# Three edits around the expert part of a decoder layer: stores of h2 and x1 from GpSimd's queue, a bank for each first tile, columns for each index product

## The chip, the cores and the metric

The kernel runs on one core of a Trainium2 chip. The metric is the device time of one execution in microseconds. A core has five engines that run side by side, each through its own list of instructions in order: TensorE (PE, matmul), VectorE (DVE), ScalarE (ACT), GpSimd (POOL) and SyncE (SP). They meet at semaphores. SyncE and GpSimd also issue transfers (DMAs), which 16 DMA engines carry out. Matmul results go to eight banks.

## The reference

The layer takes 512 tokens of 1024 channels. A mixer (a state-space branch and a forgetting-attention branch, merged by gates) is followed by a layer norm; its result is `x1`. A modulated norm of it, `h2`, goes to a mixture of 16 experts: a router picks one of four groups for each token and two experts in it.

```
for e in range(N_EXPERTS):
    hid = jax.nn.silu(t @ w_gate[e]) * (t @ w_up[e])
    out = out + gates[:, e:e + 1] * (hid @ w_down[e])
```

Here `t` holds rows of h2, an expert has 512 hidden channels, and the output is the layer norm of ALPHA times x1 plus the gated sum of the experts.

## The kernel before

Up to about 540 us the kernel computes the modulation and the mixer; the change does not touch that part. What follows is the router and the experts.

**Rows of h2 and x1.** Tokens come in four blocks of 128 rows. For blocks 0 to 2, `norms(i)` computes h2 and stores it to `h2d` in device memory, `keep_x1(i)` scales x1 and stores it to `moed`, both from SyncE's queue. For block 3 this is done by `keep_x1(3)` and `last_h2()`. SyncE's queue also issues the loads of expert weights (`ew.load`, L358): pieces of 1 MB into a ring of 19 pieces, six for an expert (two of gate, two of up, two of down). A piece is loaded again when `drop` frees it.

**Setup.** `setup_experts()` lays out the experts' buffers over memory that earlier parts leave free; GpSimd fills seven of them with zeros (L1130). Some lie where block 3's h2 rows were, and must wait for these rows' store.

**Tokens of a tile.** An expert's tokens are taken in tiles of 64. `tokens()` finds them: small matmuls of one-hot rows (L1149, L1151; "index products") give the row numbers and gates of a tile in columns 128 to 132 of bank 7. VectorE turns them into an index (L1153) and adds up the gate (L1158); GpSimd gathers the rows from `h2d` by an indirect transfer (L1154). `x_columns` transposes them (L1173, L1174).

**An expert's tile.** `body(e, t)` multiplies with gate and up weights (`up`, L1278) into bank 0 for an even t and bank 1 for an odd one, applies the activation (`hidden`), multiplies the tile before it with its down weights (`down`, L1293), scales the result (`add`, L1297) and scatters it onto `moed` by an indirect transfer that adds (L1298), transposes the hidden values (`hidden_columns`, L1287), and at t = 0 makes the index products of the expert after next. Tile 0 is always run; tiles 1 and 2 stand under branches on the expert's count (L1344, L1346). In this run's data ten experts have one tile, four have two and two have three. The work of further tiles (`over`) isn't run.

**Order.** A scheduler orders each engine's list by what it takes to be ready. Inside `in_order(...)` the order of TensorE, VectorE and ScalarE is that of the code. At a branch each engine reads the count and jumps for itself; on the path that skips tiles TensorE first waits for its own matmuls.

The end (L1405 on) loads `moed` again, normalises it and stores the output from GpSimd (L1423).

Of the kernel before, what the change touches and what calls it, by code (L numbers as in the profile page):

```python
# [14 lines left out]
ALU = mybir.AluOpType  # L15
AX = mybir.AxisListType

P = 128
# [89 lines left out]
def hybrid_layer(ctx: ExitStack, tc: tile.TileContext, A, out):  # L108
    nc = tc.nc
# [3 lines left out]
    banks = [psp.tile([P, 512], F32, name=f"bank{i}") for i in range(8)]  # L113
# [9 lines left out]
    h2d = tc.dram_tile([S, D], F32, name="h2d")  # L123
    moed = tc.dram_tile([S + P, D], F32, name="moed")
# [68 lines left out]
    for hh in range(2):  # L193
        half = slice(hh * 64, (hh + 1) * 64)
# [209 lines left out]
    for j in range(4):  # L404
        raws = [mod_pair(j, kh) for kh in range(2)] if j else mod0
        acc = FM.alloc(1)
        for k in range(KT):
            r = raws[k // 4].v(4, 512)[:, k % 4, :]
# [154 lines left out]
    for g in range(4):  # L563
# [58 lines left out]
        for c in (1, 2):  # L622
# [4 lines left out]
                                    op=ALU.add)  # L627
        for t in range(2):
# [5 lines left out]
            for hh in range(2):  # L634
                h = 2 * j + hh
                M = sums_of.pop(h)
                half = slice(hh * 64, (hh + 1) * 64)
# [47 lines left out]
    for j in range(8):  # L685
        nc.vector.scalar_tensor_tensor(gun[j].ap, gun[j].ap, cols[:, 104 + j:105 + j], ssq.ap,
                                       op0=ALU.mult, op1=ALU.mult)
# [11 lines left out]
    for j in range(4):  # L699
# [14 lines left out]
        for hh in range(2):  # L714
            m = FM.alloc(1)
            nc.vector.tensor_tensor(m.v(NT, P), fr[hh].v(NT, P), negm[:, None, :].to_broadcast([P, NT, P]),
                                    op=ALU.subtract)
# [4 lines left out]
        for i in range(NT):  # L722
# [5 lines left out]
            for (hh, hs), ps in zip(heads, pss):  # L728
                L = FM.alloc(1)
                fq = fcs[:, i, 2 * j + hh:2 * j + hh + 1]  # L730
                if i:
                    nc.vector.scalar_tensor_tensor(L.ap[:, 0:i * P], ps[:, 0:i * P], fq, fr[hh].ap[:, 0:i * P],
                                                   op0=ALU.add, op1=ALU.subtract)
                nc.vector.scalar_tensor_tensor(L.ap[:, i * P:w], ps[:, i * P:w], fq, fm_[hh].ap[:, i * P:w],
                                               op0=ALU.add, op1=ALU.subtract)
# [107 lines left out]
    for j in range(8):  # L843
        for y in (ys[j], ya[j]):
            pt = proj(hT, KT)
            t = FM.alloc(1)
# [41 lines left out]
    half = rtile("half", [P, 1])  # L888
# [6 lines left out]
    aux = rtile("aux", [P, NT, NE, 5], BF16)  # L895
# [110 lines left out]
    def norms(i):  # L1006

        r, mv = xrs[i], cp.tile([P, 8], F32, name=f"mv_{i}")
        h2s[i] = FM.alloc(2)
        h2, junk = h2s[i].v(D), jk.v(D)  # L1010
        for hf in range(2):
            hs = slice(hf * 512, (hf + 1) * 512)
            nc.vector.tensor_tensor(h2[:, hs], wps[i][hf], gt1[:, hs], op=ALU.mult)
        nc.vector.scalar_tensor_tensor(r, r, ALPHA, h2, op0=ALU.mult, op1=ALU.add, accum_out=mv[:, 0:1])
        for n, (dst, gain, bias, acc) in enumerate(((r, ln1g, ln1b, mv[:, 4:5]), (h2, sc2, sh2, None))):
            m_, v_ = mv[:, 4 * n + 1:4 * n + 2], mv[:, 4 * n + 2:4 * n + 3]
            nc.vector.tensor_scalar(m_, mv[:, 4 * n:4 * n + 1], -1.0 / D, None, op0=ALU.mult)
            nc.scalar.activation(junk, r, AF.Square, bias=m_, accum_out=v_)
            nc.scalar.activation(v_, v_, AF.Sqrt, bias=epsc, scale=1.0 / D)
            nc.vector.scalar_tensor_tensor(h2, r, m_, gain, op0=ALU.add, op1=ALU.mult)  # L1020
            nc.vector.reciprocal(v_, v_)
            if acc is not None:
                nc.vector.scalar_tensor_tensor(dst, h2, v_, bias, op0=ALU.mult, op1=ALU.add, accum_out=acc)
            else:
                nc.vector.scalar_tensor_tensor(dst, h2, v_, bias, op0=ALU.mult, op1=ALU.add)
        nc.sync.dma_start(h2d[i * P:(i + 1) * P, :], h2)

    def transposed(i):
        h2Ts[i] = FM.alloc(2)
# [15 lines left out]
    def keep_x1(i):  # L1045
        r = xrs[i]
        nc.scalar.mul(r, r, ALPHA)
        nc.sync.dma_start(moed[i * P:(i + 1) * P, :], r)

    ET = mybir.EngineType  # L1050
    i3, h3 = NT - 1, [slice(hf * 512, (hf + 1) * 512) for hf in range(2)]
# [28 lines left out]
    def last_h2():  # L1080

        h23.append(FM.alloc(2))
        h2, h2T = h23[0].v(D), h2Ts[i3].v(D)
        for hf, hs in enumerate(h3):
            pt = tr.get()
            for k in range(4 * hf, 4 * hf + 4):
                nc.tensor.transpose(pt[:, k % 4 * P:(k % 4 + 1) * P], h2T[:, k * P:(k + 1) * P], ident)
            nc.scalar.copy(h2[:, hs], pt)
        nc.sync.dma_start(h2d[i3 * P:(i3 + 1) * P, :], h2)

    def last_logits():
        t = t3[0].v(D)
# [13 lines left out]

    bgu, bys, bhid, bix = banks[0:2], [banks[2], banks[6]], banks[5], banks[7]
    h2d2 = h2d.rearrange("s (h d) -> (s h) d", h=2)  # L1110
    moed2 = moed.rearrange("s (h d) -> (s h) d", h=2)
    xgs, xTs, sgs, yos, ohs = {}, {}, [], [], []
# [30 lines left out]
        for c in range(NT):  # L1143
            nc.vector.tensor_scalar(oh[:, c, :], slots, ranks[:, c:c + 1], None, op0=ALU.is_equal)

    def tokens(oh, au, ix, gw, xg, n0=0, n1=5):

        pi = bix[:, 128 + n0:128 + n1]
        nc.tensor.matmul(pi, onesb, bigb[:, n0:n1], start=True, stop=False)  # L1149
        for c in range(NT):  # L1150
            nc.tensor.matmul(pi, oh[:, c, :], au(c)[:, n0:n1], start=False, stop=(c == NT - 1))  # L1151
        if n0 == 0:
            nc.vector.tensor_scalar(ix, bix[:, 128:129], bix[:, 129:130], half, op0=ALU.add, op1=ALU.add)  # L1153
            nc.gpsimd.indirect_dma_start(out=xg, out_offset=None, in_=h2d2,  # L1154
                                         in_offset=bass.IndirectOffsetOnAxis(ap=ix[:, 0:1], axis=0),
                                         bounds_check=2 * S - 1, oob_is_err=False)
        if n1 == 5:
            nc.vector.tensor_reduce(gw, bix[:, 130:133], axis=AX.X, op=ALU.add)  # L1158

    def oh_of(e, t):  # L1160
        return ohs[t if e or t == 2 else 3 + t]
# [2 lines left out]
        onehots(oh_of(e, t), rk[:, :, e], itbs[t])  # L1164

    def tile_tokens(e, t, n0=0, n1=5):
        tokens(oh_of(e, t), lambda c: aux[:, c, e, :], ixs[e % 3][t], gws[e % 3][t], xgs[e % 2, t], n0, n1)

    def x_columns(xg, xT):

# [130 lines left out]

    def body(e, t):

        bank, by, yo, sg = bgu[t % 2], bys[t % 2], yos[t % 2], sgs[t % 2]
        with in_order((ET.PE, ET.DVE, ET.Activation)):
            if t == 0:
                if e + 2 < NE:
# [141 lines left out]
```

## Time and profile before

| | |
|---|---|
| runs | 953.35, 956.96, 959.03 us (median 956.96) |
| profiled execution | 951.62 us, span 949.9 us |
| granted TensorE clock, mean | 0.952 |
| busy: TensorE, VectorE, ScalarE, GpSimd | 832.6, 533.8, 313.9, 101.8 us |
| bytes moved by DMA | 196.46 MB, mean 207 GB/s |

The span is the profiled time from the first to the last instruction; the execution's own time is 1.7 us longer. Start times below count from the span's start. In a row of the timeline the bracket at the end gives the idle time of that engine before the row, and what ended it. "DVEq L1344" is VectorE's sequencer at line 1344, a branch; "SPq" is a transfer that SyncE issues. "issue" names no releaser. Buffer numbers are left out: `bm` and `fm` are two pools of buffers in the core's memory, `bank` one of the eight banks.

### The profile page before, as it was taken

To read this page: it belongs to the slowest core of one execution; us is meant where nothing else is said; L and a number is where in the kernel's file an instruction comes from. 1 tells how busy PE (TensorE), PEld (TensorE's weight loads), DVE (VectorE), ACT (ScalarE), POOL (GpSimd) and SP (SyncE) were. 2 spreads that over 40 slices of the span, in tenths; PEclk is the share of its full clock that TensorE was granted. 3 is DMA by queue.
4 is the path that set the end of the run, shared out by engine and by line. 5 is a ranking of instruction groups with operands and counts; after the bars stand their busy time and mean duration, and the time that the engine had idled before them with its cause. 6 is when DMAs were issued, how large, how long until landed. Compare 5 with 4: busy or idle time off the path is not lost.

```text
span 949.9 us, 11826 instructions
## 1 busy us (share of the span) xinstructions
PE 832.6 (88%) x4216; PEld 545.7 (57%) x4216; DVE 533.8 (56%) x1310; ACT 313.9 (33%) x561; POOL 101.8 (11%) x110
## 2 busy tenths in 40 slices
PE   2899989999999999999999963899888999999830
PEld 1778778887666677888888851334343333333410
DVE  6859888868876779867656871322332322222213
ACT  5447887455544334332242431101010110010102
POOL 1001000000000000000000002212222221221211
PEclk9999999999999999999999956999999999999975
DMA  9942546313225278894534595698899988559545
GB/s 290 334 137 87 168 135 166 100 34 90 90 71 112 90 259 247 253 260 134 161 104 178 202 390 217 248 334 284 276 387 386 391 301 260 171 167 345 192 107 117
DMA packets 137409, 196.46 MB, mean 207 GB/s; under 512 B 11802, under 2 KB 85706, under 8 KB 137312
## 3 DMA queue, kind: packets, MB, share of 16 engines
q1 hardware_dynamic: 128000, 178.48, 55.7%
q0 software_dynamic: 9152, 16.88, 7.8%
q8 instruction: 46, 0.75, 0.3%
q14 instruction: 35, 0.29, 0.1%
q10 hardware_dynamic: 176, 0.06, 0.0%
HBM read 190.61 MB, written 15.25 MB: 217 GB/s over the span
## 4 chain that ended last, share of the span: by engine, by line
PE 48%; DMA 29%; issue 12%; DVE 5%; ACT 3%; POOL 1%; SPq 0%; POOLq 0%; ACTq 0%; DVEq 0%
PE bank L398 11%; PE bank L399 10%; PE bank L400 10%; DMA fm<-h2d,rt_ix 10%; DMA moed<-fm,rt_ixl 9%; DMA moed<-fm,rt_ix 5%; PE bank L1002 5%; DMA fm<-in_w_mod 3%; PE bank L726 2%; PE bank L754 2%; DVE fm L390 2%; DMA h2d<-fm 1%; DVE fm L412 1%; PE bank L744 1%; DMA fm<-rowd 1%
## 5 line engine op out<-in xcount | busy, mean ns | idle before, releaser
L398 PE MATMUL bank<-rm,rm 128*128 128x512 f32 x512 | 205.8, 406 | 0.4 <-ACT rm L431 0.4
L400 PE MATMUL bank<-rm,rm 128*128 128x512 f32 x512 | 205.6, 402 | 0.0
L399 PE MATMUL bank<-rm,rm 128*128 128x512 f32 x512 | 205.1, 401 | 0.2 <-DVE rm L433 0.2
L1278 PE MATMUL bank<-bm,fm 128*64 128x512 f32 x472 | 118.7, 618 | 9.7 <-DVEq L1344 4.3
L234 DVE TENSOR_TENSOR rm<-fm,rm 128x1024 fp32r<-128x1024 f32 (+1 forms) x76 | 87.6, 1163 | 42.5 <-ACT rm L233 27.0
L398 PEld LDWEIGHTS bank<-rm,rm 128*128 128x128 f32 x512 | 97.7, 191 | 22.0 <-issue 3.1
L399 PEld LDWEIGHTS bank<-rm,rm 128*128 128x128 f32 x512 | 97.3, 190 | 21.6 <-issue 2.1
L400 PEld LDWEIGHTS bank<-rm,rm 128*128 128x128 f32 x512 | 97.2, 190 | 20.8 <-issue 2.3
L1283 DVE TENSOR_TENSOR fm<-fm,bank 64x512 f32<-64x512 f32 x24 | 16.6, 692 | 162.5 <-ACT fm L1282 155.5
L233 ACT CAST rm<-fm 128x1024 fp32r<-128x1024 f32 (+1 forms) x76 | 75.1, 1007 | 79.0 <-PE bank L399 58.4
L1282 ACT ACTIVATE fm<-bank 64x512 f32<-64x512 f32 x24 | 14.1, 589 | 203.5 <-PE bank L1278 203.5
L1278 PEld LDWEIGHTS bank<-bm,fm 128*64 128x64 f32 x472 | 39.5, 141 | 71.6 <-issue 67.9
L1278 PE MATMUL bank<-fm,fm 128*64 128x512 f32 x296 | 75.2, 599 | 4.9 <-DVEq L1344 2.7
L1174 ACT COPY fm<-bank 128x512 f32<-128x512 f32 x38 | 20.9, 588 | 97.6 <-PE bank L1173 97.4
L1293 PE MATMUL bank<-bm,fm 128*64 128x512 f32 x232 | 52.8, 592 | 0.0
L390 DVE SCALAR_TENSOR_TENSOR fm<-fm,cact,fm 128x256 f32<-128x256 f32 x112 | 51.2, 480 | 1.8
L1278 PEld LDWEIGHTS bank<-fm,fm 128*64 128x64 f32 x296 | 25.1, 138 | 40.6 <-issue 37.0
L1297 DVE SCALAR_TENSOR_TENSOR fm<-bank,fm,fm 128x512 f32<-128x512 f32 x24 | 18.0, 751 | 47.9 <-PE bank L1293 42.7
L1002 PE MATMUL bank<-rm,rm 128*128 128x512 f32 x192 | 44.2, 391 | 0.3 <-ACT fm L847 0.3
L1298 POOL DMA_INDIRECT moed<-fm,rt_ixl x16 | 25.7, 1604 | 162.3 <-DVE fm L1297 162.3
L1154 POOL DMA_INDIRECT fm<-h2d,rt_ix x38 | 39.2, 1032 | 24.3 <-DVE fm L1158 16.3
L1002 PEld LDWEIGHTS bank<-rm,rm 128*128 128x128 f32 x192 | 36.0, 188 | 8.1 <-ACT fm L847 0.7
(309 smaller groups left out, 1088.7 us busy)
## 6 DMA issues: line engine op xcount, KB each, us to landing
bm<-in_w_down SPq DMA_DIRECT2D x20, 1024.0 KB
bm<-in_w_up SPq DMA_DIRECT2D x20, 1024.0 KB
bm<-in_w_gate SPq DMA_DIRECT2D x20, 1024.0 KB
fm<-in_w_in SPq DMA_DIRECT2D x36, 512.0 KB
fm<-in_w_mod SPq DMA_DIRECT2D x16, 1024.0 KB
fm<-in_w_up SPq DMA_DIRECT2D x12, 1024.0 KB
fm<-in_w_down SPq DMA_DIRECT2D x12, 1024.0 KB
fm<-in_w_gate SPq DMA_DIRECT2D x12, 1024.0 KB
```

The costliest lines, as they stand in the source:

```text
L233: ins = nc.scalar.copy(hi, src)
L234: nc.vector.tensor_tensor(lo, src, hi.bitcast(F32), op=ALU.subtract)
L390: nc.vector.scalar_tensor_tensor(acc, r, cact[:, k:k + 1], acc, op0=ALU.mult, op1=ALU.add)
L398: nc.tensor.matmul(pt, whi[:, k, :], ah.ap, start=(k == 0), stop=False)
L399: nc.tensor.matmul(pt, whi[:, k, :], al.ap, start=False, stop=False)
L400: nc.tensor.matmul(pt, wlo[:, k, :], ah.ap, start=False, stop=(k == nk - 1))
L1002: nc.tensor.matmul(wps[i][hf], sta.ap[:, tsl], mov.ap[:, hf * 512:(hf + 1) * 512], start=(k == 0 and sta is mh and mov is wh), stop=(k == ...
L1154: nc.gpsimd.indirect_dma_start(out=xg, out_offset=None, in_=h2d2, in_offset=bass.IndirectOffsetOnAxis(ap=ix[:, 0:1], axis=0), bounds_check ...
L1174: nc.scalar.copy(xT, pt)
L1278: nc.tensor.matmul(bank[n * H:(n + 1) * H], xT[:, (2 * (k % 4) + k // 4) * H:(2 * (k % 4) + k // 4 + 1) * H], w, start=(k == 0), stop=(k = ...
L1293: nc.tensor.matmul(bank[n * H:(n + 1) * H], hidT[0][:, k, :], w, start=(k == 0), stop=(k == 3))
L1298: nc.gpsimd.indirect_dma_start(out=moed2, in_=yo, in_offset=None, compute_op=ALU.add, out_offset=bass.IndirectOffsetOnAxis(ap=ix[:, 0:1], ...
```

## The change

Stores to `h2d` and `moed` are issued by GpSimd in place of SyncE. The banks of `up` become 0, 1, 1 for tiles 0, 1, 2, where they were 0, 1, 0. The index products of a tile stand at columns 128 + 8(3(e mod 2) + t) of bank 7, where all stood at 128. New lines shift later line numbers by two or three: L1278 becomes L1281, L1149 becomes L1151, L1154 becomes L1156, L1130 becomes L1132, L1344 becomes L1347.

```
--- before.py
+++ after.py
@@ -1023,7 +1023,7 @@
                 nc.vector.scalar_tensor_tensor(dst, h2, v_, bias, op0=ALU.mult, op1=ALU.add, accum_out=acc)
             else:
                 nc.vector.scalar_tensor_tensor(dst, h2, v_, bias, op0=ALU.mult, op1=ALU.add)
-        nc.sync.dma_start(h2d[i * P:(i + 1) * P, :], h2)
+        nc.gpsimd.dma_start(h2d[i * P:(i + 1) * P, :], h2)
 
     def transposed(i):
         h2Ts[i] = FM.alloc(2)
@@ -1045,7 +1045,7 @@
     def keep_x1(i):
         r = xrs[i]
         nc.scalar.mul(r, r, ALPHA)
-        nc.sync.dma_start(moed[i * P:(i + 1) * P, :], r)
+        nc.gpsimd.dma_start(moed[i * P:(i + 1) * P, :], r)
 
     ET = mybir.EngineType
     i3, h3 = NT - 1, [slice(hf * 512, (hf + 1) * 512) for hf in range(2)]
@@ -1086,7 +1086,7 @@
             for k in range(4 * hf, 4 * hf + 4):
                 nc.tensor.transpose(pt[:, k % 4 * P:(k % 4 + 1) * P], h2T[:, k * P:(k + 1) * P], ident)
             nc.scalar.copy(h2[:, hs], pt)
-        nc.sync.dma_start(h2d[i3 * P:(i3 + 1) * P, :], h2)
+        nc.gpsimd.dma_start(h2d[i3 * P:(i3 + 1) * P, :], h2)
 
     def last_logits():
         t = t3[0].v(D)
@@ -1106,7 +1106,9 @@
 
 
 
-    bgu, bys, bhid, bix = banks[0:2], [banks[2], banks[6]], banks[5], banks[7]
+
+
+    bgu, bys, bhid, bix = (banks[0], banks[1], banks[1]), [banks[2], banks[6]], banks[5], banks[7]
     h2d2 = h2d.rearrange("s (h d) -> (s h) d", h=2)
     moed2 = moed.rearrange("s (h d) -> (s h) d", h=2)
     xgs, xTs, sgs, yos, ohs = {}, {}, [], [], []
@@ -1143,19 +1145,19 @@
         for c in range(NT):
             nc.vector.tensor_scalar(oh[:, c, :], slots, ranks[:, c:c + 1], None, op0=ALU.is_equal)
 
-    def tokens(oh, au, ix, gw, xg, n0=0, n1=5):
-
-        pi = bix[:, 128 + n0:128 + n1]
+    def tokens(oh, au, ix, gw, xg, n0=0, n1=5, at=128):
+
+        pi = bix[:, at + n0:at + n1]
         nc.tensor.matmul(pi, onesb, bigb[:, n0:n1], start=True, stop=False)
         for c in range(NT):
             nc.tensor.matmul(pi, oh[:, c, :], au(c)[:, n0:n1], start=False, stop=(c == NT - 1))
         if n0 == 0:
-            nc.vector.tensor_scalar(ix, bix[:, 128:129], bix[:, 129:130], half, op0=ALU.add, op1=ALU.add)
+            nc.vector.tensor_scalar(ix, bix[:, at:at + 1], bix[:, at + 1:at + 2], half, op0=ALU.add, op1=ALU.add)
             nc.gpsimd.indirect_dma_start(out=xg, out_offset=None, in_=h2d2,
                                          in_offset=bass.IndirectOffsetOnAxis(ap=ix[:, 0:1], axis=0),
                                          bounds_check=2 * S - 1, oob_is_err=False)
         if n1 == 5:
-            nc.vector.tensor_reduce(gw, bix[:, 130:133], axis=AX.X, op=ALU.add)
+            nc.vector.tensor_reduce(gw, bix[:, at + 2:at + 5], axis=AX.X, op=ALU.add)
 
     def oh_of(e, t):
         return ohs[t if e or t == 2 else 3 + t]
@@ -1164,7 +1166,8 @@
         onehots(oh_of(e, t), rk[:, :, e], itbs[t])
 
     def tile_tokens(e, t, n0=0, n1=5):
-        tokens(oh_of(e, t), lambda c: aux[:, c, e, :], ixs[e % 3][t], gws[e % 3][t], xgs[e % 2, t], n0, n1)
+        tokens(oh_of(e, t), lambda c: aux[:, c, e, :], ixs[e % 3][t], gws[e % 3][t], xgs[e % 2, t], n0, n1,
+               128 + 8 * (e % 2 * 3 + t))
 
     def x_columns(xg, xT):
 
@@ -1301,7 +1304,7 @@
 
     def body(e, t):
 
-        bank, by, yo, sg = bgu[t % 2], bys[t % 2], yos[t % 2], sgs[t % 2]
+        bank, by, yo, sg = bgu[t], bys[t % 2], yos[t % 2], sgs[t % 2]
         with in_order((ET.PE, ET.DVE, ET.Activation)):
             if t == 0:
                 if e + 2 < NE:
```

GpSimd's list where the setup of the experts begins, before: `fm_78` holds h2 of block 3, `rt_ix` are the indices of a tile, `fm_81` the first tile's rows.

```order
L531 DMA fm_78<-rowd 128x512
L1130 MEMSET fm_74 128x512
L1130 MEMSET fm_75 128x512 x2
L1130 MEMSET fm_74 128x512
L1130 MEMSET fm_81 128x512
L1130 MEMSET fm_78 128x512 x2
L1154 DMA fm_81<-h2d,rt_ix_3491 128x512
L1154 DMA fm_75<-h2d,rt_ix_3492 128x512
```

The same place of GpSimd's list now, from the last store of the first three blocks:

```order
L1026 DMA h2d<-fm_70 128x1024
L1132 MEMSET fm_75 128x512
L1132 MEMSET fm_74 128x512
L1132 MEMSET fm_75 128x512
L1132 MEMSET fm_74 128x512
L1132 MEMSET fm_81 128x512
L1048 DMA moed<-fm_71 128x1024
L1089 DMA h2d<-fm_78 128x1024
L1132 MEMSET fm_78 128x512 x2
L1156 DMA fm_81<-h2d,rt_ix_3491 128x512
```

All eight stores have gone into this list, six of them ahead of the memsets. The two of block 3 stand between five memsets and the two that wait for it.

SyncE's list at the same place, before:

```order
L358 DMA bm_3762<-in_w_up 128x4x512
L358 DMA bm_3763<-in_w_gate 128x4x512
L358 DMA fm_76<-in_w_down 128x2x1024
L1048 DMA moed<-fm_71 128x1024
L1089 DMA h2d<-fm_78 128x1024
L358 DMA fm_71<-in_w_gate 128x4x512
```

The two stores of block 3 stood behind twelve loads of weights that follow one another, and one load followed them; in the list now the loads stand alone.

TensorE's list at the end of an expert (here the seventh), with what each row waits for; first the path that skips a tile, and the next expert's first rows, before. "PE_49" is TensorE's own semaphore, "DVE_49" VectorE's, "Activation_49" ScalarE's, "DMAHW" those of loads.

```order
L1346 UNCONDITIONAL_BRANCH
L1346 UNCONDITIONAL_BRANCH [waits PE_49]
L1344 UNCONDITIONAL_BRANCH [waits PE_49]
L1278 MATMUL bank_61<-bm_3753,fm_75 64x512 [waits DMAHW7_49,DVE_49,Activation_49]
L1278 MATMUL bank_61<-bm_3754,fm_75 64x512 [waits DMAHW0_49]
```

Now, from the expert's second index product, through the branch, to the next expert:

```order
L1151 LDWEIGHTS fm_80
L1151 MATMUL bank_68<-fm_80 128x5 [waits DVE_49]
...
L1281 MATMUL bank_61<-bm_3753,fm_75 64x512 [waits DMAHW7_49,Activation_49]
L1340 TENSOR_LOAD rt_cnti
L1347 COMPARE_AND_BRANCH
...
L1349 UNCONDITIONAL_BRANCH [waits PE_49]
L1347 UNCONDITIONAL_BRANCH [waits PE_49]
L1281 MATMUL bank_61<-bm_3754,fm_75 64x512 [waits DMAHW0_49]
```

The first row of the next expert's `up` has moved ahead of the branch, and no row of it waits for VectorE. The second index product waits for VectorE as it did. From the sixth expert on one row has moved in this way. In the first five experts two rows or more have moved, and the first of them stands ahead of the second index product; the fourth expert's list is, now:

```order
L1281 MATMUL bank_61<-bm_3754,fm_81 64x512 [waits DMAHW5_49,Activation_49]
L1151 LDWEIGHTS fm_80
L1151 MATMUL bank_68<-fm_80 128x5 [waits DVE_49]
...
L1281 MATMUL bank_61<-bm_3755,fm_81 64x512 [waits DMAHW6_49]
L1281 MATMUL bank_61<-bm_3754,fm_81 64x512
L1281 MATMUL bank_61<-bm_3755,fm_81 64x512
L1281 MATMUL bank_61<-bm_3754,fm_81 64x512
L1340 TENSOR_LOAD rt_cnti
L1347 COMPARE_AND_BRANCH
```

Five rows of the fifth expert's `up` stand ahead of the fourth one's branch here, where none stood before.

## Rows read from the trace of the kernel before

**Rows 1.** The page, part 1: busy time, share of the span and instructions of each engine.
```profile
PE 832.6 (88%) x4216; PEld 545.7 (57%) x4216; DVE 533.8 (56%) x1310; ACT 313.9 (33%) x561; POOL 101.8 (11%) x110
```
**Rows 2.** The page, part 4: the chain that ended last, by line.
```profile
PE bank L398 11%; PE bank L399 10%; PE bank L400 10%; DMA fm<-h2d,rt_ix 10%; DMA moed<-fm,rt_ixl 9%; DMA moed<-fm,rt_ix 5%; PE bank L1002 5%; DMA fm<-in_w_mod 3%; PE bank L726 2%; PE bank L754 2%; DVE fm L390 2%; DMA h2d<-fm 1%; DVE fm L412 1%; PE bank L744 1%; DMA fm<-rowd 1%
```
**Rows 3.** TensorE's waits, 586 to 915 us: waited for, us in total, times, longest.
```profile
PE bank L1173 <- DMA fm<-h2d,rt_ix: 20.5, 1, 20.5
...
PE bank L1149 <- issue: 6.0, 9, 0.7
PE bank L1149 <- DVE fm L1158: 5.4, 12, 0.7
...
PE bank L1278 <- ACT fm L1174: 0.6, 2, 0.3
PE bank L1278 <- issue: 0.4, 1, 0.4
```
**Rows 4.** The page, part 5: L1278's two groups (busy, mean ns, idle before, releaser).
```profile
L1278 PE MATMUL bank<-bm,fm 128*64 128x512 f32 x472 | 118.7, 618 | 9.7 <-DVEq L1344 4.3
...
L1278 PE MATMUL bank<-fm,fm 128*64 128x512 f32 x296 | 75.2, 599 | 4.9 <-DVEq L1344 2.7
```
**Rows 5.** Timeline of all engines, 554 to 590 us (start, length, engine, what).
```profile
555.20 1.09 ACT L1047 ACTIVATE fm<-fm 128x1024 f32<-128x1024 f32 x1
...
557.84 0.53 POOL L1130 MEMSET fm<- 128x512 f32 x1 [4.85 <-PE bank L1087]
...
558.62 0.59 ACT L1088 COPY fm<-bank 128x512 f32<-128x512 f32 x1 [0.27 <-PE bank L1087]
...
562.72 0.28 DVE L1153 TENSOR_SCALAR rt_ix<-bank,fm 128x1 int32<-128x1 f32 x1 [0.28 <-PE bank L1151]
...
564.60 4.10 SPq L1048 DMA_DIRECT2D moed<-fm  x1
...
568.79 0.59 SPq L1089 DMA_DIRECT2D h2d<-fm  x1
...
581.20 0.99 POOL L1130 MEMSET fm<- 128x512 f32 x2 [22.84 <-DMA h2d<-fm]
582.37 1.10 POOL L1154 DMA_INDIRECT fm<-h2d,rt_ix  x1 [0.17 <-POOL fm L1130]
583.77 1.03 POOL L1154 DMA_INDIRECT fm<-h2d,rt_ix  x1 [0.30 <-issue]
...
587.49 2.95 PE L1278 MATMUL bank<-fm,fm 128*64 128x512 f32 x10
```
**Rows 6.** Windows: length, busy of PE, PEld, DVE, ACT, POOL; clock, DMA share, GB/s.
```profile
560.00:565.00 5.00, 3.44 (x22) 1.84 (x21) 4.17 (x25) 0.00 (x0) 0.00 (x0) 0.50 1.04 406
```
**Rows 7.** The source line L1423: GpSimd's output stores of 512 KB.
```profile
L1423 POOL DMA_DIRECT2D out<-bm x4: 857/879/947, 929.5 to 936.9; - x4
...
DMA to landing us min/median/max: 8.2/8.2/8.2
```
**Rows 8.** The source line L1154 in 680 to 765 us: gathers beside weight loads.
```profile
L1154 POOL DMA_INDIRECT fm<-h2d,rt_ix x11: 1001/1041/1082, 682.5 to 746.1; - x11
...
DMA to landing us min/median/max: 6.5/6.5/6.5
```
**Rows 9.** The source line L1154 in 582 to 590 us: the first four gathers.
```profile
DMA to landing us min/median/max: 2.3/2.3/2.3
```
**Rows 10.** TensorE's timeline, 640 to 760 and 760 to 915 us: first matmuls of experts.
```profile
643.16 7.09 PE L1278 MATMUL bank<-fm,fm 128*64 128x512 f32 x32 [0.62 <-DVEq L1346]
...
683.37 8.78 PE L1278 MATMUL bank<-bm,fm 128*64 128x512 f32 x32 [1.36 <-DVEq L1344]
...
729.94 7.09 PE L1278 MATMUL bank<-bm,fm 128*64 128x512 f32 x32 [1.37 <-DMA fm<-in_w_gate]
...
792.29 7.09 PE L1278 MATMUL bank<-bm,fm 128*64 128x512 f32 x32
```
**Rows 11.** SyncE's queue in 695 to 731 us: the load of up weights used at 729.94.
```profile
702.69 2.26 SPq L358 DMA_DIRECT2D bm<-in_w_up  x1
```

More of the change, by code (lines that the diff above doesn't have):

```diff
@@ L1025, in norms @@
                 nc.vector.scalar_tensor_tensor(dst, h2, v_, bias, op0=ALU.mult, op1=ALU.add)
-        nc.sync.dma_start(h2d[i * P:(i + 1) * P, :], h2)
+        nc.gpsimd.dma_start(h2d[i * P:(i + 1) * P, :], h2)
     def transposed(i):
@@ L1047, in keep_x1 @@
         nc.scalar.mul(r, r, ALPHA)
-        nc.sync.dma_start(moed[i * P:(i + 1) * P, :], r)
+        nc.gpsimd.dma_start(moed[i * P:(i + 1) * P, :], r)
     ET = mybir.EngineType
@@ L1088, in last_h2 @@
             nc.scalar.copy(h2[:, hs], pt)
-        nc.sync.dma_start(h2d[i3 * P:(i3 + 1) * P, :], h2)
+        nc.gpsimd.dma_start(h2d[i3 * P:(i3 + 1) * P, :], h2)
     def last_logits():
@@ L1103, in last_logits @@
             nc.tensor.matmul(blg3[:, 0:20], h2T[:, k * P:(k + 1) * P], wr[:, k, :], start=(k == 0), stop=(k == KT - 1))
-    bgu, bys, bhid, bix = banks[0:2], [banks[2], banks[6]], banks[5], banks[7]
+    bgu, bys, bhid, bix = (banks[0], banks[1], banks[1]), [banks[2], banks[6]], banks[5], banks[7]
     h2d2 = h2d.rearrange("s (h d) -> (s h) d", h=2)
@@ L1144, in onehots, with tokens @@
             nc.vector.tensor_scalar(oh[:, c, :], slots, ranks[:, c:c + 1], None, op0=ALU.is_equal)
-    def tokens(oh, au, ix, gw, xg, n0=0, n1=5):
-        pi = bix[:, 128 + n0:128 + n1]
+    def tokens(oh, au, ix, gw, xg, n0=0, n1=5, at=128):
+        pi = bix[:, at + n0:at + n1]
         nc.tensor.matmul(pi, onesb, bigb[:, n0:n1], start=True, stop=False)
@@ L1152, in tokens @@
         if n0 == 0:
-            nc.vector.tensor_scalar(ix, bix[:, 128:129], bix[:, 129:130], half, op0=ALU.add, op1=ALU.add)
+            nc.vector.tensor_scalar(ix, bix[:, at:at + 1], bix[:, at + 1:at + 2], half, op0=ALU.add, op1=ALU.add)
             nc.gpsimd.indirect_dma_start(out=xg, out_offset=None, in_=h2d2,
@@ L1157, in tokens @@
         if n1 == 5:
-            nc.vector.tensor_reduce(gw, bix[:, 130:133], axis=AX.X, op=ALU.add)
+            nc.vector.tensor_reduce(gw, bix[:, at + 2:at + 5], axis=AX.X, op=ALU.add)
     def oh_of(e, t):
@@ L1166, in tile_tokens @@
     def tile_tokens(e, t, n0=0, n1=5):
-        tokens(oh_of(e, t), lambda c: aux[:, c, e, :], ixs[e % 3][t], gws[e % 3][t], xgs[e % 2, t], n0, n1)
+        tokens(oh_of(e, t), lambda c: aux[:, c, e, :], ixs[e % 3][t], gws[e % 3][t], xgs[e % 2, t], n0, n1,
+               128 + 8 * (e % 2 * 3 + t))
     def x_columns(xg, xT):
@@ L1302, in body @@
     def body(e, t):
-        bank, by, yo, sg = bgu[t % 2], bys[t % 2], yos[t % 2], sgs[t % 2]
+        bank, by, yo, sg = bgu[t], bys[t % 2], yos[t % 2], sgs[t % 2]
         with in_order((ET.PE, ET.DVE, ET.Activation)):
```

## The prediction

> **What bounds the kernel now.** I read the page first: TensorE is busy for 832.6 of 949.9 us [rows 1], so its idle time is what can be won. The chain that ended last puts a tenth of the span on the gather of token rows out of `h2d` and lists the store into `h2d` too [rows 2]. So the waits come next. TensorE's longest one in the expert part is 20.5 us, once, for that gather; the rest are short and come again with every expert: 6.0 us in 9 and 5.4 us in 12 waits before an index product [rows 3]. Before the first matmul of an expert the two groups of L1278 show 9.7 and 4.9 us of idle time [rows 4]. Of these 14.6 us, 0.6 belong to a copy and 0.4 to no releaser [rows 3]; 13.6 us are 13 waits at expert ends, nine of 0.8 to 1.4 us where the expert had one tile and four of 0.62 us where it had two. The two experts with three tiles have none.
>
> Then the timeline around the long wait [rows 5]. The last rows of h2 are complete when ScalarE's second L1088 copy ends, at 559.21. SyncE is then busy with weight loads; it issues the `moed` rows at 564.60 for 4.10 us and the `h2d` rows at 568.79. GpSimd's last memsets stand in the memory of these rows and wait for the store to land: they start at 581.20, the first gather at 582.37, the second at 583.77, the first expert's matmuls at 587.49. The indices of the first two gathers were ready at 563.0. So from 559.2 to 581.2 the program waits for one 512 KB store that stands behind others. DMA engines are full meanwhile, at 406 GB/s [rows 6].
>
> **Start of the experts (term A).** The change takes eight stores off SyncE and puts them on GpSimd, whose order is then: stores of blocks 0 to 2, five memsets, `moed` of block 3, `h2d` of block 3, two memsets, gathers. The early stores wait for norms long done by then, and cost no time there. `moed`'s rows are ready at 556.3 (L1047), and the last early memset ends at 558.37 [rows 5]. A plain store takes GpSimd 0.88 us at the end of the program [rows 7], so `moed` is issued until 559.3 and `h2d` from 559.3. Landing under a full DMA load is not shown for GpSimd's plain stores. From below: its gathers land in 6.5 us under full load, at half the bytes [rows 8]. From above: SyncE's store took 12.4 us from its issue to the memset it released (568.79 to 581.20) [rows 5]. I take 8.2 us, what GpSimd's stores of the same 512 KB take at the end [rows 7]: nearest in kind and size, and between the two. It lands at 567.5 (565.8 to 571.7). Memsets and the gap to the gather are 1.2 us as before: gather at 568.7, the second 1.4 later at 570.1. The second gather now meets the weight stream: 6.5 us instead of 2.3 [rows 8, 9], so 576.6; then 1.1 us of transposes: first matmul at 577.7 against 587.49. **A = 9.8 us**, with ends: 4.4 (store 12.4) and 15.7 (store 6.5, gathers 2.3).
>
> A rule of the Trainium skill speaks against any gain here: "DMA: Bandwidth & Descriptors", section "Rules for kernel authors", says that spreading transfers over issuing engines doesn't help, since all run on the same 16 engines; only sequencer issue time is saved. The rows show that issue time is most of what is lost (559.2 to 568.8), so the rule leaves the gain standing; if the shared engines made the store as slow as SyncE's, A would be the lower end above. The gathers take GpSimd 1.10 us beside an idle VectorE and at most 1.08 us in the stretch where VectorE builds one-hot rows beside them [rows 5, 8]. "SBUF — State Buffer", section "SBUF: two separate sides", warns that GpSimd can't write descriptors while VectorE runs a two-port copy, which would stretch both stores; no row here shows it, and VectorE's work at 558 to 560 is on tiny tiles.
>
> SyncE's loads move up past eight stores. What is loaded stays the same, and the DMA engines are full until about 580 either way, so I count nothing for it. Two loads whose memory held rows of `x1` now wait for a store of GpSimd instead of one of their own queue; the later of them is first used by the fourth expert, at 643.16, 56 us after the first one begins [rows 5, 10], so nothing for that either.
>
> **Expert ends (term B).** Before, the first matmul of the next expert shares its bank with tile 2, is bound to VectorE's passage of the branch and waits for it. With tile 2 in bank 1 that wait is gone; one to five rows of the next `up` (0.44 us each: 7.09 us for 32 records, two to a row [rows 10]) even stand ahead of the branch. What remains is TensorE's own passage: on the path that skips tiles it still waits for its own matmuls and jumps. The trace doesn't show that price alone. It lies between 0 and 0.62, since after two-tile experts the whole gap is 0.62 us [rows 10]; I take 0.45, nearer that row because the same jumps are in it. 13.6 − 13 × 0.45 = 7.8 us (ends 5.6 and 13.6). At the last expert's end the down matmuls still need VectorE's columns (0.7 us, kept).
>
> The columns: the next index product still waits for VectorE's reading of the one before in the changed program, which has the same bank in use; 14 waits of 0.67 us stay, and I give the edit itself nothing. But for the first five experts one hoisted row stands inside that wait: 5 × 0.43 = 2.2 us. And of the six third products (0.44 us each) all have a hoisted row ahead of them: 2.6 us. **B = 7.8 + 2.2 + 2.6 = 12.6 us** (10.4 to 18.4).
>
> **Clock (term C).** After three of the nine long gaps the granted clock halves for a while: the `up` at 683.37 takes 8.78 us, where the one at 729.94 takes 7.09 after the same gap [rows 10]. So one costs 1.7 us and three 5.1. The two-tile end at 643.16, with its 0.62 us, is followed by a full-speed 7.09 [rows 10]. With gaps of half a microsecond I expect most of it gone, and keep one us for what may stay: **C = 4 us**, ends 0 and 5.1.
>
> **Sum.** 9.8 + 12.6 + 4 = 26.4 us; ends 14.8 and 39.2. The profiled execution took 951.62 us, its span 949.9: 925.2 us after. The median of the runs shown is 956.96, 5.3 above it, and the same offset gives 930.5. I predict **930.5 us**; the likeliest case's own range is 918 to 942.
>
> **Rivals.**
> 1. The store doesn't come sooner: GpSimd's queue starts it at once, but DMA engines serve it after the weight stream that was queued ahead. That stream runs until about 580, so A falls to 2. For it: the full DMA row [rows 6] and SyncE's 12.4 us. Against it: gathers of 6.5 us amid the same load [rows 8]. 951.6 − (2 + 12.6 + 4) + 5.3 = 938. Chance 0.15. By the rule of "DMA: Bandwidth & Descriptors" in the Trainium skill, named above, it would come out near this figure.
> 2. The expert ends don't shrink, because TensorE's own branch takes as long as VectorE's; only the hoisted rows in waits count: 9.8 + 2.2 + 2.6 = 14.6, with no clock gained, so 951.6 − 14.6 + 5.3 = 942. For it: VectorE's release is only inferred from semaphore events. Against it: three-tile ends without any gap (792.29) [rows 10]. Chance 0.15.
> 3. Slower: the hoisted matmuls stand ahead of tiles 1 and 2 in TensorE's order and wait for weights of the next expert that aren't there, while tile 1 could run. The place is the six experts with several tiles. It decides from 26.4 + 4.8 = 31 us, over 5.2 us for each; with 7.5 us each it is 951.6 − 26.4 + 45 + 5.3 = 975. Against it: the weights used at 729.94 were issued up to 702.69 [rows 10, 11], some 27 us ahead, more than twice SyncE's 12.4. An earlier start shortens that by at most A. Chance 0.04.
> 4. The change does little: 1 and 2 together, 951.6 − (2 + 4.8) + 5.3 = 950, and within the measurement if the offset is less. Chance 0.05.
>
> The forecast itself has 0.61. About 0.5% (4.8 us) is what a measurement of this kernel tells from none. Faster by more: 0.61 + 0.15 + 0.15 and nearly half of rival 4, 0.92; within: 0.04; slower: 0.04. The range takes in the forecast's own 918 to 942 and a little beyond for rival 2 and for a store that lands with the gathers: 915 to 944.
>
> **What would show it.** Right: the last `h2d` store issued on GpSimd near 559, memsets near 567.5, first expert matmul near 578; gaps at expert ends of about half a microsecond, 0.67 us still ahead of second products from the sixth expert on, and no half-clock `up` after them. Wrong: memsets after 575 (rival 1), gaps of 1.3 us that no VectorE row releases (rival 2), hoisted matmuls that wait for a load (rival 3). If second index products start without their 0.67 us, my reading of the columns is wrong and the kernel gains up to 7 us more.

## The result, and the profile after

The changed kernel took 940.86 us (median of 4 runs, 938.57 to 941.35) against 955.15 us of the kernel before on the same chip (4 runs, 953.35 to 959.03): a ratio of 0.984, interval 0.980 to 0.988, some 15 us. The profiled execution took 941.18 us, its span is 939.3 us. That is inside the predicted range of 915 to 944, and 10.4 us above the predicted 930.5. The gain of 26.4 us that the prediction added up did not come; a little over half of it did, and about two thirds of that from the first of its three terms.

The start of the experts first. These are rows of the timeline of all engines in the changed kernel, from 554 to 592 us (start, length, engine, what, and in brackets the idle time before and what ended it):

```profile
558.54 1.09 ACT L1047 ACTIVATE fm<-fm 128x1024 f32<-128x1024 f32 x1
...
560.80 9.52 SPq L358 DMA_DIRECT2D bm<-in_w_gate  x1
...
561.73 0.53 POOL L1048 DMA_DIRECT2D moed<-fm  x1
561.96 0.59 ACT L1088 COPY fm<-bank 128x512 f32<-128x512 f32 x1 [0.27 <-PE bank L1087]
562.84 0.53 POOL L1089 DMA_DIRECT2D h2d<-fm  x1 [0.58 <-ACT fm L1088]
...
571.85 0.98 POOL L1132 MEMSET fm<- 128x512 f32 x2 [8.48 <-DMA h2d<-fm]
...
573.00 1.10 POOL L1156 DMA_INDIRECT fm<-h2d,rt_ix  x1 [0.17 <-POOL fm L1132]
574.41 1.04 POOL L1156 DMA_INDIRECT fm<-h2d,rt_ix  x1 [0.30 <-issue]
...
579.10 2.09 PE L1176 MATMUL bank<-ident,fm 128*128 128x128 f32 x8 [10.66 <-DMA fm<-h2d,rt_ix]
...
581.12 5.91 PE L1281 MATMUL bank<-fm,fm 128*64 128x512 f32 x17
```

GpSimd issues the store at 562.84, 0.3 us after ScalarE's copy ends at 562.55; SyncE is in the middle of a load that it takes 9.52 us to issue, and nobody waits for it. The memsets follow 9.0 us after the issue, where they followed 12.4 us after SyncE's [rows 5]. From the end of the copy to the first expert's matmul it is 18.57 us, where it was 28.28: the store is issued 9.3 us sooner after the copy and lands, by the memsets that it releases, 3.4 us sooner after its issue, and from the memsets to the first matmul it now takes 9.27 us, where it took 6.29. The program as a whole stood 3.3 us later than before at this point (558.54 against 555.20 for L1047). That comes from the part before 500 us, which the change does not touch, and it is not stable: in a second profile of the changed kernel the same row stands at 557.03.

Then TensorE's waits in the expert part, 576 to 905 us (waited for, us in total, times, longest), to be held against [rows 3, 4]:

```profile
PE bank L1176 <- DMA fm<-h2d,rt_ix: 10.7, 1, 10.7
PE bank L1151 <- DVE fm L1160: 6.8, 12, 0.7
PE bank L1281 <- issue: 1.9, 1, 1.9
PE bank L1281 <- PEq L1349: 1.3, 3, 0.4
PE bank L1281 <- PEq L1347: 1.1, 7, 0.2
...
PE bank L1281 <- DMA bm<-in_w_up: 0.4, 1, 0.4
```

The 13.6 us of waits for VectorE at expert ends have shrunk to 2.8 us with TensorE's own sequencer's or a load's name on them, and of 12.8 us ahead of index products (14 waits of 0.67, six of 0.44, three of 0.25) 6.8 are left. By this list 16.8 us are gone from the expert part, against one new stop of 1.9 (before there was one of 0.4). But from the first expert's first matmul to the last expert's down matmuls it is 316.64 us (581.12 to 897.76), where it was 320.26: 3.6 us less. A list of waits says what TensorE waited for, not what it lost. Its timeline at the end of a one-tile expert, 699 to 717 us, shows where the rest is:

```profile
699.75 0.17 PE L1151 MATMUL bank<-fm 128*128 128x5 bf16 x1
699.78 0.24 PE L1153 MATMUL bank<-fm,fm 128*128 128x5 bf16 x4
700.69 0.17 PE L1151 MATMUL bank<-fm 128*128 128x5 bf16 x1 [0.67 <-DVE fm L1160]
700.72 0.24 PE L1153 MATMUL bank<-fm,fm 128*128 128x5 bf16 x4
700.88 1.07 PE L1281 MATMUL bank<-bm,fm 128*64 128x512 f32 x2
702.11 6.62 PE L1281 MATMUL bank<-bm,fm 128*64 128x512 f32 x29 [0.15 <-PEq L1347]
708.18 0.59 PE L1296 MATMUL bank<-fm,fm 128*64 128x512 f32 x1
708.57 0.59 PE L1281 MATMUL bank<-bm,fm 128*64 128x512 f32 x1
```

The row that was moved ahead of the branch (two records at 700.88) takes 1.07 us. The 15 rows behind the jump take 7.05 us (702.11 to 709.16), and 7.09 is what all 16 took [rows 10]. A row has been taken out of the run, and the run has not become shorter. The gap of 1.36 us is filled with a row that saves nothing.

### The profile page after: what moved, and what is told of

It reads as the page before. It is cut to its first block, busy times and chain, and to the rows that moved or that the text cites. A ratio compares the mean times of both kernels' runs of the same rounds, so it can differ in the third digit from the quotient of the medians.

```text
span 939.3 us, 11850 instructions
## 1 busy us (share of the span) xinstructions
PE 845.4 (90%) x4216; PEld 544.4 (58%) x4216; DVE 534.7 (57%) x1310; ACT 313.6 (33%) x561; POOL 105.8 (11%) x118
## 5 line engine op out<-in xcount | busy, mean ns | idle before, releaser
L1281 PE MATMUL bank<-bm,fm 128*64 128x512 f32 x472 | 124.2, 597 | 1.8 <-PEq L1347 0.8
L1281 PE MATMUL bank<-fm,fm 128*64 128x512 f32 x296 | 81.4, 610 | 3.8 <-issue 1.9
L1281 PEld LDWEIGHTS bank<-bm,fm 128*64 128x64 f32 x472 | 38.1, 136 | 66.7 <-issue 65.4
L1296 PE MATMUL bank<-bm,fm 128*64 128x512 f32 x232 | 60.4, 592 | 0.0
L1281 PEld LDWEIGHTS bank<-fm,fm 128*64 128x64 f32 x296 | 24.7, 140 | 40.7 <-issue 39.0
L1156 POOL DMA_INDIRECT fm<-h2d,rt_ix x38 | 39.1, 1029 | 28.7 <-DVE fm L1160 20.6
## 6 DMA issues: line engine op xcount, KB each, us to landing
bm<-in_w_down SPq DMA_DIRECT2D x20, 1024.0 KB, 13.7
```

Source lines behind the costliest of these rows:

```text
L1281: nc.tensor.matmul(bank[n * H:(n + 1) * H], xT[:, (2 * (k % 4) + k // 4) * H:(2 * (k % 4) + k // 4 + 1) * H], w, start=(k == 0), stop=(k = ...
L1296: nc.tensor.matmul(bank[n * H:(n + 1) * H], hidT[0][:, k, :], w, start=(k == 0), stop=(k == 3))
```

## The experiments

I measure an expert from its last transposes of hidden values (L1287 before, L1290 after) to the next one's; this leaves out the start and what happened earlier. The one-tile expert below runs at full clock and without a further stop; in the changed kernel it is one from the sixth on.

| kernel | one tile, us | two tiles, us | ratio to before |
|---|---|---|---|
| before | 14.39 | 25.82 | 1 |
| changed | 14.13 (13.58 to 13.64 among the first five) | 26.13 (25.56 in the first half) | 0.984 |
| e5_hold | 13.82 to 13.91 | 25.73 | 0.986 |
| e6_pair | 12.83 to 12.90 | 25.14 | 0.971 |
| e7_bank1 | 12.51 | 25.09 | 0.974 |
| e8_three_banks | 12.51 | 24.35 | 0.966 |
| e9_bank1_pair | 12.60 | 24.96 | 0.966 |

**The parts alone.** e1_stores has the change's lines at L1026, L1048 and L1089 and nothing else; e2_banks its banks; e3_columns its columns.

```
-        nc.sync.dma_start(h2d[i3 * P:(i3 + 1) * P, :], h2)          # e1, and two more
+        nc.gpsimd.dma_start(h2d[i3 * P:(i3 + 1) * P, :], h2)
-        bank, by, yo, sg = bgu[t % 2], ...                            # e2
+        bank, by, yo, sg = bgu[t], ...                                # bgu = banks 0, 1, 1
-        pi = bix[:, 128 + n0:128 + n1]                                # e3
+        pi = bix[:, at + n0:at + n1]                                  # at = 128 + 8 * (e % 2 * 3 + t)
```

> Only the eight stores go to GpSimd; banks and columns are as before, and TensorE's list is the same. Theory 1 (the start of the experts carries nearly the whole gain, the expert ends gave almost nothing): the time from the end of ScalarE's last h2 copy to the first expert matmul falls from 28.3 to about 18.6 us as in the changed kernel, gaps at expert ends stay 0.6 to 1.4 us, and the ratio to the kernel before is 0.987 to 0.991 (about 9 to 12 us). Rival (the ends gave half of the change's 14 us): the same start, but the ratio is 0.993 or more, since the start can then have given only 7.

Measured: 943.92 us, ratio 0.990 (0.987 to 0.994), 9.4 us. The end of the copy to the first matmul is 18.78 us (558.79 to 577.57). The stores alone give the whole of term A. Whether it is GpSimd's queue that does it, or only the place ahead of the twelve loads, which SyncE could have given too, no run takes apart.

> Only the banks of up become 0, 1, 1. Theory 1: the gaps at expert ends shrink from 1.36 to 0.15 us, but the one row of up that is moved ahead of the branch takes 1.07 us by itself where a row in a run of rows takes 0.43, so a one-tile expert without a clock drop takes 14.1 us instead of 14.4 and a two-tile expert 26.1 instead of 25.8; with the clock drops gone the ratio is 0.992 to 0.999 (1 to 7 us). Rival (the prediction's term B: 0.45 us for the own branch, hoisted rows cost nothing): 12 us and the clock's 4, a ratio of 0.983.

Measured: 949.84 us, ratio 0.995 (0.993 to 0.997), 5 us. One-tile experts 14.13 us, two-tile ones 26.15, as in the changed kernel. The rival's 16 us are excluded.

> Only the index products get columns of their own; stores and banks are as before. Theory (the wait hangs on the bank): the 0.67 us before second products stays, and the ratio is 0.997 to 1.003. Rival (columns of their own let the product go ahead): the 14 waits go, ratio 0.990.

Measured: 956.78 us, ratio 1.000 (0.998 to 1.003). The waits of 0.67 us all stand. Columns of their own do nothing, as predicted. The three parts add up within their intervals: by the ratios 9.4 and 4.8 and nothing make 14.2 of the 15.

**The change again.**

> The changed kernel once more, for a second profile and for times beside the experiments. Theory: ratio 0.982 to 0.987; the start of the experts 9.7 us sooner after ScalarE's last h2 copy than before, one-tile experts of the second half 14.1 us, a stop of about 2 us in the last expert's up again. Rival (that stop, and the slow first up, were accidents of one execution): they are absent, and the expert part is 2 to 3 us shorter.

Measured: 940.78 us, ratio 0.983 (0.979 to 0.988); the copy's end to the first matmul 18.62 us, one-tile experts 14.13 us. The slow first up and the stop in the last expert are there again: they are no accident of one execution.

**What the moved row costs.** In e5_hold the first row of the next up is bound behind the tiles under the branch, by order alone.

```
+            if t == 0 and e:
+                first = <first TensorE instruction of this up>
+                tc.add_manual_dep(first, last_pe[e - 1, 1], <order only>)
```

> The changed kernel, with the first row of an expert's up bound in TensorE's order behind the tiles under the branch, so that no row is moved ahead of it; it still waits for no VectorE branch. Theory 1 (a row of gate and a row of up run side by side, and an odd row moved ahead runs alone and is drained before the jump): the gap at the end of a one-tile expert is 0.2 to 0.6 us with no lone row, such an expert takes 13.3 to 13.7 us instead of 14.1, a two-tile one 25.6 instead of 26.1, and the ratio is 0.972 to 0.979 against 0.984 of the changed kernel. Rival (the moved row is harmless, what remains is the branch itself): the gap grows by what the row took, and the ratio stays at 0.984.

Measured: 940.61 us, ratio 0.986 (0.982 to 0.990). My theory had the right sign and the wrong size: one-tile experts 13.82 to 13.91 us, not 13.3 to 13.7 (two more took 14.25 and 14.49), and the medians of the two kernels can't be told apart. In the profiled execution what the ends save is lost elsewhere: the second expert takes 18.67 us, where it takes 13.79 in the changed kernel, with a stop of 2.61 us in the up behind it and half the clock after the stop, and a later one 15.64, again at half clock. TensorE's timeline at such an end in e5_hold:

```profile
674.76 0.17 PE L1151 MATMUL bank<-fm 128*128 128x5 bf16 x1
...
675.69 0.17 PE L1151 MATMUL bank<-fm 128*128 128x5 bf16 x1 [0.67 <-DVE fm L1160]
675.72 0.24 PE L1153 MATMUL bank<-fm,fm 128*128 128x5 bf16 x4
676.76 7.09 PE L1281 MATMUL bank<-bm,fm 128*64 128x512 f32 x32 [0.80 <-PEq L1355]
```

With nothing moved, TensorE's own passage is 0.80 us here, released by its own sequencer, and 0.72 to 1.24 us at the nine one-tile ends, where the prediction took 0.45 and 0.62 for the most.

e4_gate_then_up asks whether rows of an up run one after the other at all. It is the kernel before, with the eight gate rows first and the eight up rows behind them.

```
-        for k in range(KT):
-            for n, w in enumerate(strm.up(e, k)):
+        for n in range(2):
+            for k in range(KT):
+                w = strm.up(e, k)[n]
```

> The kernel before, with the order of rows inside up changed: all eight rows of gate and then all eight of up, where they alternate. Same rows, same banks. Theory (a row of gate fills one half of TensorE's columns and one of up the other, and two that alternate run side by side): an up takes 13 to 14 us in place of 7.09, and with 24 of them the kernel is 150 us slower or more, some 1100 us. Rival (rows follow one another at 0.43 us whatever half they use): 7.1 us and no change.

Measured, one run: 1080.93 us, 124 us more, and 5.2 us more in each of the 24 tiles. An up in its timeline (the last rows of it lie beside rows of down, L1294):

```profile
763.51 10.97 PE L1279 MATMUL bank<-bm,fm 128*64 128x512 f32 x29 [1.38 <-DVEq L1345]
773.90 0.64 PE L1294 MATMUL bank<-fm,fm 128*64 128x512 f32 x1
774.32 0.59 PE L1279 MATMUL bank<-bm,fm 128*64 128x512 f32 x1
774.38 0.59 PE L1294 MATMUL bank<-fm,fm 128*64 128x512 f32 x1
```

An up takes 12 us instead of 7.09 with the same rows. So a gate row (results in one half of the bank's partitions) and an up row (in the other) run side by side when they alternate. The Trainium skill describes this for small matmuls packed into one array ("TensorE: Matmul & The Clock Gate", section "Part 3: Packing small matmuls — row/col tiling"), and the run agrees. It is not that a gate row and its up row share the same tokens' columns: where the order changes from gate to up, rows of different columns meet and run side by side too, so that the first 29 records take 10.97 us, where one after another, at 0.43 us each, they would take over 12. The last ones pair with rows of down. The 0.44 us a row that the prediction got by dividing holds for pairs only. It came out less than the 150 us I had expected, since I had left these pairs at the border out.

e6_pair moves two rows, a gate row and an up row, to the place between the two index products.

```
+                if e + 2 < NE:
+                    tile_tokens(e + 2, 0)
+                up(ew, e + 1, xTs[1 - e % 2, 0], bgu[0], 0, 1)      # rows of k = 0
+                if e + 2 < NE:
+                    tile_tokens(e + 2, 1)
```

> As e5_hold, but the first two rows of the next expert's up, one of gate and one of up, are written between the two index products of an expert's end. Theory 1 (only an odd row costs): the pair takes 0.86 to 1.1 us of which 0.67 fill the wait of the second product, so a one-tile expert takes 13.2 to 13.5 us against 13.85 of e5_hold, a two-tile one 25.2 to 25.5, and the ratio is 0.975 to 0.982 against 0.986. Rival (any row of up that is drained before the jump costs its full length): 13.8 us or more, and 0.986.

Measured: 929.68 us, ratio 0.971 (0.966 to 0.976). TensorE's timeline at the end of a one-tile expert:

```profile
668.05 0.17 PE L1151 MATMUL bank<-fm 128*128 128x5 bf16 x1
668.08 0.24 PE L1153 MATMUL bank<-fm,fm 128*128 128x5 bf16 x4
668.25 1.08 PE L1281 MATMUL bank<-bm,fm 128*64 128x512 f32 x4
669.26 0.18 PE L1151 MATMUL bank<-fm 128*128 128x5 bf16 x1
669.30 0.24 PE L1153 MATMUL bank<-fm,fm 128*128 128x5 bf16 x4
669.93 6.23 PE L1281 MATMUL bank<-bm,fm 128*64 128x512 f32 x28 [0.39 <-PEq L1358]
```

Two rows take 1.08 us where one took 1.07 us, they stand in the wait of the second product, and the 14 rows behind the jump take 6.23 us. Against the changed kernel a one-tile expert is 1.2 to 1.3 us shorter, and with 12.83 to 12.90 us shorter than the 13.2 I had expected for the least. The passage of the branch has also shrunk, from 0.80 to 0.39 us, where no wait stands just ahead of it.

**What the wait of the second product hangs on.** e7_bank1 is e5_hold with the index products of tile 1 in bank 1.

```
-               128 + 8 * (e % 2 * 3 + t))
+               128 + 8 * (e % 2 * 3 + t), banks[1] if t == 1 else bix)
```

> As e5_hold, and the index products of tile 1 are written to bank 1 in place of bank 7, so that a second product no longer has the bank that VectorE reads from. Theory (the wait hangs on the bank, not on the columns): the 0.67 us waits ahead of second products go, 14 of them and so 9 us below e5_hold, ratio 0.962 to 0.970. Rival (the 0.67 us is what VectorE's chain takes, and comes back as a wait of the branch or of the next up row): the ratio is that of e5_hold within 0.003.

Measured: 928.42 us, ratio 0.974 (0.970 to 0.978), 12 us below e5_hold and so more than expected. The same end in its timeline, and the longest of three stops of over 1.1 us, one expert later:

```profile
681.75 0.17 PE L1151 MATMUL bank<-fm 128*128 128x5 bf16 x1
681.78 0.24 PE L1153 MATMUL bank<-fm,fm 128*128 128x5 bf16 x4
681.88 0.17 PE L1151 MATMUL bank<-fm 128*128 128x5 bf16 x1
681.91 0.24 PE L1153 MATMUL bank<-fm,fm 128*128 128x5 bf16 x4
682.45 7.44 PE L1281 MATMUL bank<-fm,fm 128*64 128x512 f32 x32 [0.30 <-ACTq L1355]
...
698.41 9.82 PE L1281 MATMUL bank<-bm,fm 128*64 128x512 f32 x32 [3.39 <-PEq L1355]
```

The second product follows the first at once, and the gap at the branch is 0.30 us. The wait for VectorE did not come back elsewhere at these ends. One bank took away both waits, the one ahead of the product and most of the branch's. Why the branch is passed sooner, the rows of TensorE's sequencer show (PEldq; the lengths in ns, then the start), of e5_hold in 675 to 677 us and of e7_bank1 in 680 to 683 us:

```profile
L1348 PEldq TENSOR_LOAD <-rt_cnti x1: 305/305/305, 675.7 to 675.7; - x1
L1355 PEldq COMPARE_BRANCH  x1: 333/333/333, 676.1 to 676.1; - x1
```
```profile
L1348 PEldq TENSOR_LOAD <-rt_cnti x1: 298/298/298, 680.9 to 680.9; - x1
L1355 PEldq COMPARE_BRANCH  x1: 325/325/325, 681.3 to 681.3; - x1
```

In e5_hold the sequencer stands at the second product's wait until 675.69; only then does it read the count and jump, and the first row of up follows 1.07 us after the wait. In e7_bank1 nothing holds it there: it reads the count at 680.9 and jumps while TensorE is still busy with transposes and products, which end at 682.15, and up starts at 682.45.

For the wait ahead of the product the Trainium skill has the reason ("PSUM — Partial Sum Buffer", section "PSUM bank collisions raise a hardware error"): two engines may not be on the same bank and partitions at a time, whatever the columns, and the compiler's scheduler adds a wait for it. The rows of e3_columns and e7_bank1 agree: 0.67 us with other columns, none with another bank. e10_bank0 puts the cause to the test from the other side: tile 2's products, made and read under the branch, go to bank 0, the bank of the next first up.

> As e7_bank1, with tile 2's index products in bank 0, the bank of the next expert's first up. Theory (the wait for VectorE at expert ends in the kernel before came from a bank that VectorE reads under the branch): the first up of an expert waits for VectorE's branch again, 0.9 to 1.4 us at one-tile ends in place of 0.30, one-tile experts 13.2 to 13.8 us. Rival (the wait came from tile 2's up alone): 12.5 us as in e7_bank1.

Measured, one run: 938.45 us, one-tile experts 14.25 us. TensorE's timeline:

```profile
675.15 8.66 PE L1281 MATMUL bank<-bm,fm 128*64 128x512 f32 x32 [2.04 <-DVEq L1355]
690.98 8.78 PE L1281 MATMUL bank<-fm,fm 128*64 128x512 f32 x32 [2.03 <-DVEq L1355]
```

The wait for VectorE's branch is back at 2.04 us, which is as much as the 0.67 and the 1.36 us of the kernel before together. On the path that was run VectorE reads none of tile 2's products; that it might is enough. I had expected 0.9 to 1.4, forgetting that the first of the two waits would now come due here.

**Further.** e8_three_banks writes the products of tiles 0, 1, 2 to banks 7, 6, 2; e9_bank1_pair joins e6 and e7.

> As e5_hold, with the index products of tiles 0, 1, 2 in banks 7, 6 and 2: tile 1's and tile 2's stand in banks of down that are idle then. Theory (a wait on a bank that VectorE reads, whatever the columns): the 0.67 us waits ahead of second products go as in e7_bank1, and of the waits ahead of third products and of tile 1's up at expert ends under the branch (0.5 to 0.7 us, six times) most go too; one-tile experts 12.5 us, two-tile ones 24.6 to 24.9 against 25.1, ratio 0.968 to 0.974. Rival (VectorE's chain itself is what these wait for, and the wait moves to the next instruction): two-tile experts stay at 25.1.

> e6_pair and e7_bank1 together: a pair of up rows of the next expert between the two index products, and tile 1's products in bank 1. Theory: both take away the same 0.67 us, so there is little left to add; the pair only covers TensorE's own passage of the branch (0.30 us in e7_bank1), one-tile experts 12.2 to 12.6 us, ratio 0.968 to 0.975. Rival (the two add up): one-tile experts below 12.0 us and a ratio of 0.96.

Measured: 926.58 us, ratio 0.966 (0.963 to 0.969), and 926.22 us, ratio 0.966 (0.964 to 0.969). In e8 the waits under the branch go too (two tiles 24.35 us), a little beyond what I expected; in e9 the two edits do not add up, as the theory had it, since both take away the same wait. Both beat the kernel before by 32 us and, by the ratios, the changed one by some 16. What is next shows in e8 at 700.45, in TensorE's timeline; behind it the window of 685 to 695 us (length, busy time of five engines, granted clock, DMA share, GB/s), the landing of weight loads (L358) in 660 to 716 us, the jump of TensorE's sequencer in 696 to 701 us, and, of the DMA queues in 697.6 to 697.7 us, the one that brings instructions (packets, MB, share):

```profile
700.45 10.01 PE L1281 MATMUL bank<-bm,fm 128*64 128x512 f32 x32 [2.81 <-PEq L1355]
```
```profile
685.00:695.00 10.00, 9.38 (x46) 4.02 (x44) 2.97 (x16) 0.59 (x1) 2.32 (x3) 1.00 1.05 386
```
```profile
DMA to landing us min/median/max: 13.6/15.2/17.1
```
```profile
L1355 PEldq COMPARE_BRANCH  x1: 3336/3336/3336, 696.8 to 696.8; - x1
```
```profile
q8 instruction: 1, 0.02, 69.6%
```

The DMA engines are full and a weight load takes some 15 us to land; SyncE issues one at 684.73, which would be there at about 700, where this up starts. But the stop is not one for weights: the first two rows of this up wait for loads issued at 670.10 and 671.88, whose semaphores had been complete since 682.56 and 685.26. What the trace shows beside the stop (697.64 to 700.45) is the jump itself, which takes 3.34 us here and 0.33 at the end before (683.4), and a packet of 16 KB of instructions that starts at 697.65. Before 520 us TensorE starts 254 matmuls and weight loads on average from one such packet to the next, so I take the queue for TensorE's. In the eight profiles with the new banks, e10_bank0 apart, TensorE stops for over 1.1 us ahead of a row of up 16 times, whatever name the row bears, and each of these stops ends 2.2 to 2.9 us after such a packet began, of which there are some 25 in 320 us. So I read them as waits for TensorE's own instructions; no run moves the code to prove it.

## Why the prediction came out as it did

**Term A** (9.8 us at the start) was right, and by its own steps. The interval from the copy to the first matmul fell by 9.7 us; the store took 9.0 us to land where I took 8.2 from [rows 7], the issue 0.53 us where I took 0.88, and the second gather landed in 5.6 us where I took the 6.5 of [rows 8], a single landing. So it is luck that these small errors cancel. The full DMA engines delay GpSimd's store no more than that, so rival 1 is out. In e1_stores the interval falls by 9.5 us by the stores alone. Two slips of the prediction did no harm: with its own steps a store of 12.4 us leaves a gain of 5.6 us and not 4.4, and the late issue, 9.6 of the 22.0 us from the copy to the memsets, was less than half of what was lost and not most of it.

**Term C** (4 us of clock) came out at 4.1 us, in part by luck: the three slow ups of before, 5.3 us by the experts' lengths (1.9, 1.7 and 1.7), are gone, as forecast. The first up of all, of which the prediction does not speak, gives 1.2 back. It spends 5.91 us on the 17 records that took 4.66: the mean granted clock is 0.65 from 581 to 586 us, where it was 0.86 from 587 to 592 before, so it stays longer at the lower of its two levels (1.2 and 2.4 GHz). The earlier start alone doesn't explain that: in e6_pair and e7_bank1, which start as early, the clock is 0.83 and 0.89 over the same length of time.

**Term B** (12.6 us at expert ends) failed: of the 3.6 us that the expert part gained, 4.1 are the clock's and minus 1.5 the stop of 1.9 in place of one of 0.4, so the ends gave 1.0 us. Two steps failed. "I take 0.45": TensorE's passage of the branch is some 0.8 us where a wait stands just ahead of it (e5_hold), and only 0.30 where none does (e7_bank1). I had bounded it by the two-tile ends' 0.62, because "the same jumps are in it"; but there no index product waits ahead of the jump and the count has long been read. The bound came from another situation. The 13 gaps at the ends add up to 10.2 us in e5_hold, so that 3.5 us are saved, not 7.8. The larger miss is "0.44 us each: 7.09 us for 32 records, two to a row". That is the mean over pairs that run side by side. A row alone takes 1.07 us, and the rows left behind the jump no longer pair up as they did. So the moved rows, which I credited with 4.8 us, cost: a one-tile end of the changed kernel is 0.2 to 0.3 us longer than e5_hold's, a two-tile one 0.4, and a three-tile expert 0.5 us longer than before. Only where the moved rows stand in the first half's waits do they save something (25.56 us for two tiles there).

**The columns** were right: the wait stayed, and e3_columns measures nothing. The prediction's reason, that the bank counts, is what e7_bank1 shows; its last sentence, that up to 7 us more lay in these waits, was too low, since without them the branch is passed sooner too.

**Rival 2** was the nearest to the result, with 942 us, though its reason was only half right: the branch was passed sooner than by VectorE's pace, and something else took the time. **Rival 3**, the moved rows that wait for weights, did not come: no row ahead of a branch waits for a load. By the profiled executions the miss is 16.0 us (925.2 forecast, 941.18 measured): 11.6 of it are term B's, 3.3 come from the unsteady part ahead of the change, and 1.5 from the stop, of which the prediction does not speak. That the result lies in the range is owed to the range's upper end, drawn for rival 2, and to terms A and C; the likeliest case's own 942 holds it only just. The offset of 5.3 us to the median hid a third of the miss: the profiled execution of before was a quick one, while that of the changed kernel lies 0.3 us above its median.

## What to carry to other kernels

A wait that is gone from a list is not time won: measure the interval from one fixed instruction to the next of its kind, and see whether the work that moved into the gap still costs what it cost in its old place. Before you price an instruction by a run's length over its count, ask what ran beside it; take it out singly and it may cost its full length, and leave its partner alone. And where an engine waits for the reading of something it does not use, look at which bank both are in rather than at the columns.

## What the runs showed that I had not expected

- Two rows of 64 x 512 whose results lie in different halves of a bank took 1.08 us together, one took 1.07 us (e6_pair, the changed kernel); eight of one half in a row and then eight of the other made an up 5.2 us longer.
- TensorE's passage of a branch at a one-tile end took some 0.8 us behind a wait, 0.39 with a pair of matmuls ahead of the last product, and 0.30 us behind work that did not wait, beside which its sequencer had read the count (0.30 us) and jumped (0.33 us).
- In both profiles of the changed kernel, and in those of e2_banks, e6_pair and e9_bank1_pair, TensorE stops once in the last expert's up for about 2 us with no releaser; the changed kernel's timeline, 882 to 890 us:

```profile
882.72 1.07 PE L1281 MATMUL bank<-bm,fm 128*64 128x512 f32 x2
...
883.95 0.61 PE L1281 MATMUL bank<-fm,fm 128*64 128x512 f32 x1 [0.15 <-PEq L1347]
...
886.42 0.59 PE L1281 MATMUL bank<-fm,fm 128*64 128x512 f32 x1 [1.86 <-issue]
```

  In e1_stores, e5_hold, e7_bank1 and e8_three_banks a stop of 2.2 to 2.6 us with the same mark stands in the third expert's up; e6_pair and e9_bank1_pair have a shorter one there too (1.15 and 1.45 us). Each ends 2.2 to 2.7 us after a packet of instructions began (here 884.09 and 886.42), as in e8_three_banks above.
